# Ten added TensorE transposes of f32 words, two f16 numbers to a word, in the first stage of a matmul-logsumexp kernel

## The chip, the cores and the metric

The kernel runs on one core of one Trainium2 chip. The metric is device time in microseconds (us), as the median of several executions. One execution of each kernel is also taken by the hardware profiler; all numbers marked as read from the trace come from such a profile. The span in a profile (first to last instruction) is some 1.8 us shorter than the device time of the same execution.

## The reference

```python
m, k, n = 1024, 4096, 4096
a = np.random.randn(m, k).astype(np.float32)
b = np.random.randn(k, n).astype(np.float32)

def reference(a, b):
    x = np.matmul(a, b)
    return special.logsumexp(x, axis=-1).astype(np.float32)
```

## The kernel before

The kernel multiplies in f16 and works on blocks of 512 columns of b, most of them with a scheme of seven products in place of eight. Only the first stage matters here. In it, pieces of a (128 rows by 512 columns) and of b arrive by DMA, 64 arrivals in all, in groups of eight: a0, b, a1, b, a2, a3, a4, a5. Each piece of a is transposed on TensorE, four 128x128 transposes into one bank of PSUM (the memory that TensorE writes in this kernel, eight banks), and copied out to SBUF (the memory in which the operands lie), by VectorE and ScalarE in turn. There are two such banks, `tps[0]` and `tps[1]`, used in turn (`tps_99` and `tps_100` in the traces); the other six banks accumulate products.

```python
    tps = [
        psum_pool.tile([P, 2 * FD], f16, name=f"tps_{h}", tag="ps") for h in range(2)
    ]                                   # P = 128, FD = 512: each is one whole bank

    def transpose_group(k0, kn, m):     # kn = 4
        src = stg.pop((k0, m))
        n = count[0]                    # counts pieces of a only
        count[0] += 1
        pst = tps[n % 2]
        for j in range(kn):
            nc.tensor.matmul(pst[:, ts(j, P)], src[:, ts(j, P)], ident,
                             is_transpose=True, start=(j == 0), stop=(j == kn - 1))
        dst = aT[:, k0 // 2 : (k0 + kn) // 2, :, m // 2, m % 2, :]
        v = pst[:, 0 : kn * P].rearrange("p (i t c) -> p i t c", t=2, c=P)
        if n % 2 == 0:
            nc.vector.tensor_copy(out=dst, in_=v)     # L227
        else:
            nc.scalar.copy(out=dst, in_=v)            # L229

    # ... cut ...

    back = []
    for n, (k0, kn, what, x) in enumerate(arrivals):
        # ... issue of further loads, cut ...
        if what == "a":
            transpose_group(k0, kn, x)                # L216 in the profile
        if k0 < KN and x < 3:
            warm(1)                                   # matmuls of zeros, L295
        if len(back) == 1 + (n >= MT) + (n >= 4 * MT):
            behind(*back.pop(0))        # plain matmuls of an earlier arrival, L234,
        back.append((k0, kn, what, x))  # and sums of a on VectorE
        # ... cut ...

    # ... the other stages, cut ...
    nc.sync.dma_start(out=out.rearrange("(p mt) -> p mt", mt=MT), in_=lg)
```

The four transposes fill the lower half of a bank: 512 f16 of 1024. The upper half is free. In the traces of this kernel the matmuls, and the copies of each engine, run in the order in which the program names them.

Of the kernel before, what the change touches and what calls it, by code (L numbers as in the profile page):

```python
# [13 lines left out]
def kernel(  # L14
# [6 lines left out]
    nc = tc.nc  # L21
    P = 128
    FD = 512
    H = FD // 2
    f32 = mybir.dt.float32
    f16 = mybir.dt.float16
    AX = mybir.AxisListType
    ALU = mybir.AluOpType
# [6 lines left out]
    MP, KP = MT // 2, KT // 2  # L35
# [7 lines left out]
    cst_pool = ctx.enter_context(tc.tile_pool(name="cst", bufs=1))  # L43
# [14 lines left out]
            name=nc.get_next_instruction_name(),  # L58
# [7 lines left out]
    s1 = cst_pool.tile([P, KP, MP, P], f16, name="s1")  # L66
    s2 = cst_pool.tile([P, KP, MP, P], f16, name="s2")
# [15 lines left out]
    lg = cst_pool.tile([P, MT], f32, name="lg")  # L83
# [48 lines left out]
    class Block:  # L132
# [15 lines left out]
        def load(self, lo, hi):  # L148
            nc.gpsimd.dma_start(
                out=self.raw[lo // GI][:, lo % GI : lo % GI + hi - lo],  # L150
                in_=b_rows[:, lo:hi, :, ts(self.nb, FD)],
            )
# [36 lines left out]
    def acc_tiles(name):  # L189
# [6 lines left out]
    tps = [  # L196
        psum_pool.tile([P, 2 * FD], f16, name=f"tps_{h}", tag="ps") for h in range(2)
    ]
# [11 lines left out]
    def transpose_group(k0, kn, m):  # L210
        src = stg.pop((k0, m))
        n = count[0]
# [3 lines that stand above are left out]
            nc.tensor.matmul(  # L216
                pst[:, ts(j, P)],
                src[:, ts(j, P)],
                ident,
                is_transpose=True,  # L220
                start=(j == 0),
                stop=(j == kn - 1),
# [7 lines that stand above are left out]
# [40 lines left out]
    def behind(k0, kn, what, x):  # L270
        if what == "a":
            have_a.setdefault(k0, []).append(x)
            todo = [(k, x) for k in range(k0, k0 + kn) if k in have_b]
        else:
            have_b.update({k0: 1, k0 + 1: 1})
            todo = [(k, m) for k in (k0, k0 + 1) for m in have_a.get(x, [])]
        for k, m in todo:
            plain(acc[m // 2][m % 2], k // 2, k % 2, m)
        r = slice(k0 // 2, (k0 + kn) // 2)
        if what == "a":  # L280
            if x >= 3 and in_place:
                a_sums_late(*in_place.pop(0))
            if x % 2 == 1 and k0 + kn < KT:
                a_sums_early(r, x // 2)
            if x == 5:
                in_place.extend([(r, 0), (r, 1), (r, 2)])
            if k0 + kn == KT and x == 4:
                first_max(0)
                first_max(1)
                for what in ("t1", "t6"):  # L290
                    blk1.make(what, 0, 2)

    def warm(n):
        for _ in range(n):
            nc.tensor.matmul(acc[2][1], zeros[:, 0:P], zeros[:, 0:FD], start=True, stop=True)  # L295
# [21 lines left out]
    def load(k0, kn, what, x):  # L317
# [8 lines left out]
        if len(coming) == len(arrivals) - 3 * MT:  # L326
            nc.gpsimd.memset(negmax, 3.0e38)
            nc.gpsimd.memset(tsum, 0.0)

    back = []  # L330
    for n, (k0, kn, what, x) in enumerate(arrivals):
        while coming and (coming[0][2] == "b" or loads[0] < count[0] + NSLOT):
            load(*coming.pop(0))
            if not coming:
                for lo in range(0, KP, 2):
                    blk1.load(lo, lo + 2)
        if what == "a":
            transpose_group(k0, kn, x)
        if k0 < KN and x < 3:
            warm(1)  # L340
        if len(back) == 1 + (n >= MT) + (n >= 4 * MT):
            behind(*back.pop(0))
        back.append((k0, kn, what, x))
        while back and k0 < KN and what == "b":
            behind(*back.pop(0))
# [69 lines left out]
    def spread_turned():  # L415
        for g in range(4):
            for j in range(4):
                for eng, t, u in ((nc.gpsimd, tnm, negmax), (nc.gpsimd, tts, tsum)):
                    eng.tensor_copy(  # L419
                        out=u[ts(j, 32), :, WIDE[g]].rearrange("p (q r) -> p r q", r=2),  # L420
                        in_=t[ts(g, 32), 0].rearrange("p (r q j) -> p r q j", r=2, j=4)[
                            :, :, :, j
                        ],
                    )
# [86 lines left out]
    for step, (_, qs) in enumerate(plan):  # L511
# [4 lines left out]
        if more:  # L516
            if plan[step + 1][0] is again1:
                nxt = last
            else:
                nxt = plan[step + 1][0]()  # L520
                if step == 1:
# [3 lines left out]
                        out=ident[0:1, 0:2], in_=aT[0:1, 0, 0, MP - 1, :, 0]  # L525
# [23 lines left out]
        for q in qs:  # L549
# [108 lines left out]
            if final:  # L658
# [28 lines left out]
                    out=w, in_=w, func=AF.Exp, bias=n0, scale=-1.0, accum_out=l0  # L687
# [47 lines left out]
            if early and q == 1:  # L735
                last = again1().load_all()
                spread_turned()

    nc.sync.dma_start(out=out.rearrange("(p mt) -> p mt", mt=MT), in_=lg)


# [28 lines left out]
```

## Time and profile before

| | before |
|---|---|
| device time, median of the first 6 runs | 419.52 us (419.36 to 420.19) |
| span of the profile | 418.3 us |
| TensorE busy | 412.2 us |
| VectorE / ScalarE / GpSimd busy | 315.9 / 120.5 / 99.5 us |

The engines and their busy time, from the first part of the profile's page of the kernel before (PE is TensorE, PEld its weight loads, DVE VectorE, ACT ScalarE, POOL GpSimd), and the shares of the chain of work that ended last:

```profile
PE 412.2 (99%) x2747; PEld 261.4 (62%) x2747; DVE 315.9 (76%) x709; ACT 120.5 (29%) x447; POOL 99.5 (24%) x189
...
PE 97%; DMA 1%; DVE 0%; ACT 0%; issue 0%; SPq 0%; ACTq 0%
```

TensorE bounds the kernel. Its waits, longest first, in the kernel before (engine, what it was about to do, what it waited for; then us in total, times, longest):

```profile
PE acc_1_98 L295 <- DVE s_73 L298: 1.2, 1, 1.2
PE acc_0_93 L234 <- DVE aT L227: 0.6, 1, 0.6
```

Both are near the start. The stretch that the change touches comes next, as the timeline of the kernel before shows it (start, duration, engine, line, operation, output<-input, shapes, count; in brackets idle time before it and what ended it). A matmul's record ends later than the next one starts (the group of four at 27.15 has 0.39 us, and the next group starts 0.22 us after it); the text counts the distance of starts, the pitch.

```profile
27.15 0.39 PE L216 MATMUL tps_99<-ident,tb 128*128 128x128 f16 x4
...
27.37 1.03 PE L234 MATMUL acc_0_97<-b_1_86,aT 128*128 128x512 f16 x4
27.57 0.42 DVE L227 COPY aT<-tps_99 128x512 f16<-128x512 f16 x1 [0.74 <-PE tps_99 L216]
...
29.10 0.39 PE L216 MATMUL tps_100<-ident,tb 128*128 128x128 f16 x4
...
29.52 0.59 ACT L229 COPY aT<-tps_100 128x512 f16<-128x512 f16 x1 [2.45 <-PE tps_100 L216]
...
29.75 0.39 PE L216 MATMUL tps_99<-ident,tb 128*128 128x128 f16 x4
...
30.16 0.11 PEld L234 LDWEIGHTS <-aT 128*128 128x128 f16 x2 [0.19 <-ACT aT L229]
30.16 0.61 PE L234 MATMUL acc_1_94<-b_1_86,aT 128*128 128x512 f16 x2
```

Four f16 transposes take 0.22 us of pitch (27.15 to 27.37), 56 ns each. TensorE goes on at once with matmuls into other banks while VectorE copies the transposes out, until 27.99. The arrivals are 24 (27.15), 26 (29.10) and 28 (29.75); the two pieces of b between them have no transposes.

One more reading, on how the two halves of a bank are treated. First the kernel before near 116 us: c21 and c22 are the two halves of the bank `acc_1_1`. The record of the product into c21 ends at 116.04 (115.44 + 0.60); the copy L631 reads c21 alone and starts at 117.83.

```profile
115.44 0.60 PE L560 MATMUL acc_1_1_1348<-b_3_750,s_72 128*128 128x256 f16 x4
115.88 1.91 PE L560 MATMUL acc_1_1_1348<-tb,aT 128*128 128x256 f16 x16
...
117.83 0.37 ACT L631 COPY s_1_1349<-acc_1_1_1348 128x256 f32<-128x256 f32 x1 [2.86 <-PE acc_1_1_1348 L560]
```

Then the same in the last step, where c22 has a bank of its own:

```profile
405.41 1.91 PE L560 MATMUL acc_3_1_3992<-aT,s_72 128*128 128x256 f16 x16
...
407.16 1.91 PE L560 MATMUL c_3993<-tb,aT 128*128 128x256 f16 x16
407.40 0.37 ACT L631 COPY s_3_3994<-acc_3_1_3992 128x256 f32<-128x256 f32 x1 [1.20 <-PE acc_3_1_3992 L560]
```

In a shared bank the copy starts 1.79 us after the end of its own product, and 0.04 us after that of the product into the other half (115.88 + 1.91 = 117.79); with separate banks it starts 0.08 us after its own product (405.41 + 1.91 = 407.32). This program orders accesses by bank, not by address. The Trainium skill, "PSUM — Partial Sum Buffer", section "PSUM bank collisions raise a hardware error", says why a program is made so: two engines that touch one bank and the same 32 partitions at once raise an error, at different addresses too.

### The profile page before, as it was taken

Reading aid. Unit: us, or ns where it says so; the run is one execution under the profiler, and the core shown is the slowest. Engines: PE = TensorE matmul, PEld = TensorE weight load, DVE = VectorE, ACT = ScalarE, POOL = GpSimd, SP = SyncE. Lnnn points to the kernel's source line nnn. Section 1 sums busy time; section 2 is a strip of 40 time slices with the busy share of each in tenths; the row PEclk is TensorE's granted clock in tenths of the full one; section 3 lists DMA queues with packets and bytes.
Section 4 is the critical chain, followed back from the end, with each engine's and each line's share of the span. In section 5 each row is a group of like instructions: output and inputs, shape, how many; then the busy total and the mean of one; then the engine's idle time right before and its main releaser. Section 6 shows DMA issues by size and latency. Waiting matters only on the chain.

```text
span 418.3 us, 7100 instructions
## 1 busy us (share of the span) xinstructions
PE 412.2 (99%) x2747; PEld 261.4 (62%) x2747; DVE 315.9 (76%) x709; ACT 120.5 (29%) x447; POOL 99.5 (24%) x189
## 2 busy tenths in 40 slices
PE   8999999999999999999999999999999999999996
PEld 2555558888888844444444444444444468888885
DVE  2466688869646657978788896978789998299955
ACT  2222341132132210515215051512406052222124
POOL 7677753001010030013100031012200230294000
PEclk9999999999999999999999999999999999999999
DMA  9999999999999499103980089300990059699000
GB/s 183 203 202 204 203 205 207 207 207 215 190 191 179 68 163 207 33 2 48 208 148 0 2 135 207 60 1 8 201 195 2 0 86 207 112 192 207 6 2 0
DMA packets 57841, 53.28 MB, mean 127 GB/s; under 512 B 10192, under 2 KB 56912, under 8 KB 57808
## 3 DMA queue, kind: packets, MB, share of 16 engines
q0 software_dynamic: 48928, 49.95, 72.3%
q1 hardware_dynamic: 8880, 2.89, 4.2%
q8 instruction: 21, 0.34, 0.3%
q14 instruction: 12, 0.10, 0.1%
HBM read 100.66 MB, written 2.10 MB: 246 GB/s over the span
## 4 chain that ended last, share of the span: by engine, by line
PE 97%; DMA 1%; DVE 0%; ACT 0%; issue 0%; SPq 0%; ACTq 0%
PE acc_1_94 L234 2%; PE acc_0_93 L234 2%; PE acc_0_95 L234 2%; PE acc_1_0_1347 L560 2%; PE acc_1_0_767 L560 2%; PE acc_2_0_769 L560 2%; PE acc_0_0_765 L560 2%; PE acc_1_0_3395 L560 2%; PE acc_3_0_3851 L560 2%; PE acc_3_0_3715 L560 2%; PE acc_0_0_3263 L560 2%; PE acc_2_0_1482 L560 2%; PE acc_0_0_1215 L560 2%; PE acc_2_0_3579 L560 2%; PE acc_3_0_1615 L560 2%; PE wide_1_2_3078 L445 2%
## 5 line engine op out<-in xcount | busy, mean ns | idle before, releaser
L560 PEld LDWEIGHTS <-aT 128*128 128x128 f16 x832 | 81.4, 98 | 9.6
L445 PEld LDWEIGHTS <-tb 128*128 128x128 f16 x384 | 37.6, 98 | 45.1
L382 ACT ACTIVATE tb<-tb,ident 128x32 f32<-128x32 f32 x128 | 39.1, 306 | 6.4 <-DVE ident L379 6.4
L403 POOL TENSOR_TENSOR ident<-ident,tmin 128x96 f32<-128x96 f32 x8 | 3.1, 384 | 134.9 <-DVE tmin L405 134.9
L391 ACT ACTIVATE tb<-tb 128x512 f32<-128x512 f32 x8 | 5.0, 630 | 90.1 <-DVE tb L86 90.1
L205 POOL DMA_DIRECT2D tb<-in_a_dram x47 | 25.4, 544 | 7.1 <-issue 2.0
L234 PEld LDWEIGHTS <-aT 128*128 128x128 f16 x192 | 16.8, 99 | 15.2 <-DVE aT L227 1.8
L229 ACT COPY aT<-tps_100 128x512 f16<-128x512 f16 x24 | 14.1, 586 | 39.0 <-PE tps_100 L216 39.0
L227 DVE COPY aT<-tps_99 128x512 f16<-128x512 f16 x24 | 10.2, 425 | 19.7 <-PE tps_99 L216 19.7
L382 ACT ACTIVATION_READ_ACCUMULATOR tb<-tb,ident 128x1 f32 x128 | 23.9, 186 | 0.0
L216 PEld LDWEIGHTS <-tb 128*128 128x128 f16 x192 | 15.0, 100 | 12.5 <-DVE tb L309 1.0
L560 PEld LDWEIGHTS <-s_71 128*128 128x128 f16 x208 | 20.3, 98 | 2.8
L560 PEld LDWEIGHTS <-s_72 128*128 128x128 f16 x208 | 20.4, 98 | 2.4
L560 PEld LDWEIGHTS <-s_73 128*128 128x128 f16 x208 | 20.3, 98 | 2.4
L89 DVE TENSOR_TENSOR aT<-aT 128x256 f16<-128x256 f16 (+1 forms) x56 | 16.2, 343 | 0.0
L379 DVE TENSOR_REDUCE ident<-tb 128x16 f32<-128x512 f32 x16 | 11.0, 686 | 1.1
L86 DVE TENSOR_TENSOR s_71<-aT 128x256 f16<-128x256 f16 (+1 forms) x26 | 8.2, 316 | 2.5 <-ACT aT L229 2.2
L216 PE MATMUL tps_99<-ident,tb 128*128 128x128 f16 x96 | 9.5, 223 | 0.1
L216 PE MATMUL tps_100<-ident,tb 128*128 128x128 f16 x96 | 9.5, 223 | 0.0
L86 DVE TENSOR_TENSOR s_73<-aT 128x256 f16<-128x256 f16 (+1 forms) x26 | 8.3, 318 | 0.0
L86 DVE TENSOR_TENSOR s_72<-aT 128x256 f16<-128x256 f16 (+1 forms) x26 | 8.3, 317 | 0.0
L419 POOL COPY tsum<-tts 32x8 f32<-32x8 f32 x16 | 7.8, 486 | 0.0
(939 smaller groups left out, 966.7 us busy)
## 6 DMA issues: line engine op xcount, KB each, us to landing
tb<-in_a_dram POOLq DMA_DIRECT2D x47, 128.0 KB, 5.9
aT<-in_b_dram POOLq DMA_DIRECT2D x4, 1024.0 KB, 15.1
b_1_86<-in_b_dram POOLq DMA_DIRECT2D x4, 256.0 KB, 6.2
b_2_87<-in_b_dram POOLq DMA_DIRECT2D x4, 256.0 KB, 6.2
b_3_88<-in_b_dram POOLq DMA_DIRECT2D x4, 256.0 KB, 6.2
b_0_89<-in_b_dram POOLq DMA_DIRECT2D x2, 512.0 KB, 9.1
b_1_90<-in_b_dram POOLq DMA_DIRECT2D x2, 512.0 KB, 12.3
b_2_91<-in_b_dram POOLq DMA_DIRECT2D x2, 512.0 KB, 15.6
```

Source lines behind the costliest of these rows:

```text
L86: nc.vector.tensor_tensor(out=o, in0=x, in1=y, op=ALU.add)
L89: nc.vector.tensor_tensor(out=o, in0=x, in1=y, op=ALU.subtract)
L205: nc.gpsimd.dma_start(out=slot, in_=a_m[m, :, k0 * P : (k0 + kn) * P])
L216: nc.tensor.matmul(pst[:, ts(j, P)], src[:, ts(j, P)], ident, is_transpose=True, start=(j == 0), stop=(j == kn - 1),)
L227: nc.vector.tensor_copy(out=dst, in_=v)
L229: nc.scalar.copy(out=dst, in_=v)
L234: nc.tensor.matmul(pt, aT[:, i, kp, m // 2, m % 2, :], blk0.raw[i // GI][:, i % GI, kp, :], start=(done[m] == 0), stop=(done[m] == KT - 1),)
L379: nc.vector.tensor_reduce(out=nm, in_=v, axis=AX.X, op=ALU.max, negate=True)
L382: nc.scalar.activation(out=v[:, i], in_=v[:, i], func=AF.Exp, bias=nm[:, i : i + 1], accum_out=tts[:, 1 + h, r * WN // 2 + i : r * WN // 2 ...
L419: eng.tensor_copy(out=u[ts(j, 32), :, WIDE[g]].rearrange("p (q r) -> p r q", r=2), in_=t[ts(g, 32), 0].rearrange("p (r q j) -> p r q j", r ...
L445: nc.tensor.matmul(c.rearrange("p (q m) -> p q m", m=P), lhs(i), rhs(i), start=(start and i == 0), stop=(stop and i == KP - 1), skip_group ...
L560: nc.tensor.matmul(c, lhs(i), rhs(i), start=(start and i == 0), stop=(i == KP - 1), skip_group_check=True,)
```

## The change

The intent is to see what f32 transposes cost and whether they pass words unchanged. Each f32 word holds two f16 numbers, the lower 1.0 and the upper 0, so the word as an f32 is subnormal (all bits of its exponent are 0). At five arrivals two transposes of such words go into the upper half of a `tps` bank, and VectorE takes the minimum of the lower f16 numbers. At the end 1000 times that minimum less 1000 is added to the output: 0 if the words came through, far off if a lower number came out smaller. The check is narrower than the intent: each of the five reductions overwrites `seen`, so only the last, of arrival 28, reaches the output, and a minimum of the lower numbers shows neither one that came out larger nor a changed upper number.

```diff
+    word_id = s2[:, KP - 1].rearrange("p q c -> p (q c)").bitcast(f32)[:, 0:P]
+    words16 = s1[:, KP - 1].rearrange("p q c -> p (q c)")[:, 0 : 2 * P]
+    words = words16.bitcast(f32)
+    seen = cst_pool.tile([P, 1], f32, name="seen")
+
+    def words_through(n):
+        for j in range(2):
+            nc.tensor.matmul(
+                tps[n % 2].bitcast(f32)[:, 2 * P + j * P : 2 * P + (j + 1) * P],
+                words,
+                word_id,
+                is_transpose=True,
+                start=(j == 0),
+                stop=(j == 1),
+            )
+        v = tps[n % 2][:, 4 * P : 8 * P].rearrange("p (c t) -> p t c", t=2)
+        nc.vector.tensor_reduce(out=seen, in_=v[:, 0], axis=AX.X, op=ALU.min)
+
     back = []
     for n, (k0, kn, what, x) in enumerate(arrivals):
 ... cut ...
         if what == "a":
             transpose_group(k0, kn, x)
+        if n == 10:
+            make_identity(nc, word_id)
+            nc.vector.memset(words16, 0.0)
+            nc.vector.memset(words16[:, 0::2], 1.0)
+        if n in (24, 25, 26, 27, 28):
+            words_through(n)
 ... cut ...
+    nc.vector.tensor_scalar(
+        out=seen, in0=seen, scalar1=1000.0, scalar2=-1000.0, op0=ALU.mult, op1=ALU.add
+    )
+    nc.vector.tensor_scalar(
+        out=lg, in0=lg, scalar1=seen, scalar2=None, op0=ALU.add
+    )
     nc.sync.dma_start(out=out.rearrange("(p mt) -> p mt", mt=MT), in_=lg)
```

Note that `words_through` chooses its bank by the arrival's number, `transpose_group` by the count of pieces of a. So at arrivals 24 and 28 the words go into the bank that was just written and is about to be copied out; at 27 into the bank of arrival 26; at 25 and 26 into a bank that is free.

## The prediction

> **What bounds the kernel now.** TensorE. The chain of waits gives PE 97% of the span, the busy table 412.2 of 418.3 us. In the first stage (to about 62 us, 64 arrivals, a period of 6.72 us for eight) PE is solid: its waits are 1.2 and 0.6 us, both near the start. The added transposes fall in the fourth group of arrivals: by the order of matmuls in the timeline, between 27.15 and 30.6 us. Nothing later has slack, so what PE loses there moves the end one for one.
>
> **What is added, in order of size.**
>
> 1. Waits on PE. The added transposes write the upper half of a bank whose lower half is being copied out. The trace shows that the halves of a bank are ordered against each other in this program: the ScalarE copy of c21 (L631) could start when its own product ends (115.9 us), yet starts at 117.83, after the product into the other half of the bank; in the last step, where that product has its own bank, the copy starts at once (407.40 after 407.32). So I expect:
>    - arrival 24: after its four transposes the words wait for VectorE's copy of the same bank. PE would go on at 27.37; the copy ends at 27.99: about 0.67 us.
>    - arrival 28: the same, 0.67 us.
>    - arrival 27: waits for ScalarE's copy of arrival 26 (29.52 + 0.59 us): 0.84 us less the words of arrival 26. It swallows the wait of 0.19 us that is now at 30.16.
>    - arrivals 25 and 26: their banks should be free.
>    Sum: 0.67 + 0.67 + 0.84 - 0.19 = 2.0 us, less one pair of words.
> 2. The transposes. An f16 transpose has 56 ns of pitch here (four in 0.22 us). The Trainium skill, "TensorE: Matmul & The Clock Gate", Terms, says that trn2's transpose mode made FP32 four times faster, so I take one pass; its section on weight-path modes says that fast weight load is not for FP32, so the weight load (98 ns busy for f16 here) may set the pitch. Estimate: 0.12 us each, a pair w = 0.25 us. Five pairs less the one hidden: 4w = 1.0 us. No f32 matmul is in this trace. Four passes would make it 2 us or more.
> 3. Changes between f32 and f16 weights: 0.2 us, a guess.
> 4. The tail: two small VectorE instructions, the second dependent on the first, before the store. Such ones step by 0.19 us there (412.51 to 412.70). Together 0.3 us, on the chain.
>
> Off the chain: five reductions of 256 f16 from PSUM (about 0.4 us each, as the 128x256 one at 413.43), where VectorE has 4.3 us busy of 6.8; two memsets; the identity on GpSimd, 0.5 to 0.9 us, in gaps of its load issue. Nothing is removed.
>
> **Prediction.** 419.5 + 2.0 + 1.0 + 0.2 + 0.3 = 423.0 us, range 421.3 to 425.3. Faster by over 2%: 0.01; within 2%: 0.95; slower by over 2%: 0.04.
>
> The words are subnormal as f32. I expect them through unchanged (3 in 4); otherwise the output is off by 1000, at the same time.
>
> **Right if** the waits of PE show two of about 0.65 us for VectorE's L227 copies and one of about 0.6 us for ScalarE's L229 copy; the ten matmuls pitch at 60 to 130 ns; the tail is 0.3 us longer; all between keeps its length.
>
> **Wrong if** the halves of a bank are not ordered (421.3 us or less), f32 transposes take several passes or stall the weight load (over 425), or the reductions delay VectorE's copies so that later transposes wait.

## More of the kernel before

The end of the kernel before:

```profile
415.81 0.16 DVE L89 TENSOR_TENSOR lg<-lg,nmmin 128x2 f32<-128x2 f32 x1 [0.65 <-ACT lg L689]
416.00 0.35 SPq L739 DMA_DIRECT2D out_dram<-lg  x1
```

## The result, and the profile after

The changed kernel is correct. Its median is 422.66 us (422.35 to 423.93, 10 runs) against 419.62 us (418.95 to 421.06, 20 runs) of the kernel before: 3.04 us more. The ratio is 1.0074, with a 95% interval of 1.0063 to 1.0085, so 2.6 to 3.6 us.

The stretches of the two kernels, from the windows view. The first window runs from the start of the transposes of arrival 24 to the first matmul after the first stage; the second from there to the end of TensorE's work. Columns: start and end, length, then busy us (and instructions) of each engine, granted clock, DMA share, GB/s. Before:

```profile
27.15:61.67 34.52, 34.50 (x249) 19.22 (x248) 23.79 (x94) 10.44 (x20) 23.52 (x39) 1.00 1.24 204
61.67:414.35 352.68, 352.64 (x2353) 230.01 (x2351) 279.76 (x568) 101.72 (x412) 55.91 (x110) 1.00 0.70 116
```

After:

```profile
26.05:63.68 37.63, 36.05 (x259) 20.39 (x258) 25.81 (x99) 10.42 (x20) 25.10 (x41) 1.00 1.24 204
63.68:416.36 352.68, 352.64 (x2353) 230.00 (x2351) 279.45 (x568) 101.71 (x412) 55.56 (x110) 1.00 0.69 115
```

The first window is 3.11 us longer (37.63 - 34.52). All that follows up to the tail has the same length to 10 ns. TensorE has 1.58 us of idle time in the first window where it had 0.02.

The same stretch of the timeline, now of the changed kernel:

```profile
26.47 0.42 DVE L227 COPY aT<-tps_99 128x512 f16<-128x512 f16 x1 [0.74 <-PE tps_99 L216]
...
27.05 0.41 PE L337 MATMUL tps_99<-s_72,s_71 128*128 128x128 f32 x2 [0.61 <-DVE aT L227]
...
27.29 1.03 PE L234 MATMUL acc_0_97<-b_1_86,aT 128*128 128x512 f16 x4
...
28.16 0.38 PE L337 MATMUL tps_100<-s_72,s_71 128*128 128x128 f32 x2
...
29.24 0.39 PE L216 MATMUL tps_100<-ident,tb 128*128 128x128 f16 x4
...
29.46 0.39 PE L337 MATMUL tps_99<-s_72,s_71 128*128 128x128 f32 x2
...
29.66 0.58 ACT L229 COPY aT<-tps_100 128x512 f16<-128x512 f16 x1 [3.69 <-PE tps_100 L216]
...
30.30 0.44 PE L337 MATMUL tps_100<-s_72,s_71 128*128 128x128 f32 x2 [0.45 <-ACT aT L229]
...
30.57 0.59 PE L234 MATMUL acc_0_93<-b_1_86,aT 128*128 128x512 f16 x2
...
31.00 0.39 PE L216 MATMUL tps_99<-ident,tb 128*128 128x128 f16 x4
31.43 0.42 DVE L227 COPY aT<-tps_99 128x512 f16<-128x512 f16 x1 [0.17 <-PE tps_99 L216]
...
31.91 0.44 PE L337 MATMUL tps_99<-s_72,s_71 128*128 128x128 f32 x2 [0.52 <-DVE aT L227]
...
32.19 0.59 PE L234 MATMUL acc_1_94<-b_1_86,aT 128*128 128x512 f16 x2
```

The added transposes are L337. At arrival 24 (transposes from 26.05, four of them, so TensorE could go on at 26.27) the words start at 27.05, after VectorE's copy ended at 26.89: 0.78 us lost. At arrival 27 the words could start at 29.46 + 0.22 = 29.68, and start at 30.30, after ScalarE's copy: 0.62 us. At arrival 28 they could start at 31.22 and start at 31.91: 0.69 us. The old wait of 0.19 us before L234 is gone, because ScalarE's copy was waited for already. The sum is 0.78 + 0.62 + 0.69 - 0.19 = 1.90 us. The five pairs themselves take 0.24, 0.21, 0.22, 0.27 and 0.28 us from their start to the next matmul, 1.22 us (the third, behind which TensorE waits, is put at 0.22 us like the pairs in the flow). 1.90 + 1.22 = 3.12 us, which accounts for the 3.11.

The same trace holds the counterpart. The pair of arrival 26 (29.46) also comes directly behind four transposes whose copy is still to come, but goes into the other bank, which nobody reads then: it starts 0.22 us after them, without a wait. The pair of arrival 25 (28.16), whose bank is free too, does not wait either. Only the pairs whose own bank was still to be copied out waited.

The bracket of a wait is shorter (0.61, 0.45, 0.52) than the time lost, because the modelled end of the matmul before it counts as busy. The waits view of the changed kernel has the same numbers:

```profile
PE tps_99 L337 <- DVE aT L227: 1.1, 2, 0.6
PE tps_99 L216 <- DMA tb<-in_a_dram: 1.0, 2, 0.7
...
PE tps_100 L337 <- ACT aT L229: 0.5, 1, 0.5
```

Its second line is one that the profile of before did not have: transposes that waited for loads of a (`tb` holds the staged pieces). It is taken up below.

The tail of the changed kernel:

```profile
417.81 0.16 DVE L89 TENSOR_TENSOR lg<-lg,nmmin 128x2 f32<-128x2 f32 x1 [0.65 <-ACT lg L713]
417.89 0.15 DVE L763 TENSOR_SCALAR seen<-seen 128x1 f32<-128x1 f32 x1
418.07 0.23 DVE L766 TENSOR_SCALAR lg<-lg,seen 128x8 f32<-128x8 f32 x1
418.40 0.35 SPq L769 DMA_DIRECT2D out_dram<-lg  x1
```

The store follows the last subtraction by 0.59 us in place of 0.19: 0.40 us more.

So the traces say 3.11 + 0.40 = 3.51 us, and the times say 3.04 us with an interval that reaches to 3.6. The spans of the two profiles differ by only 2.4 us (420.7 - 418.3), because the changed kernel came to arrival 24 earlier by 1.10 us (26.05 against 27.15). This is not the change's doing: in the second profile of the kernel before (the last experiment) arrival 24 starts at 26.14 us, and against its span of 417.3 us the changed kernel has 3.4 us more.

### The profile page after: what moved, and what is told of

Read it like the earlier page. It is cut to its first block, busy times and chain, and to the rows that moved or that the text cites. A ratio compares the mean times of both kernels' runs of the same rounds, so it can differ in the third digit from the quotient of the medians. Undisturbed runs are those within 1.5% of the kernel's fastest.

```text
span 420.7 us, 7137 instructions
## 1 busy us (share of the span) xinstructions
PE 411.6 (98%) x2757; PEld 261.7 (62%) x2757; DVE 318.4 (76%) x718; ACT 120.5 (29%) x447; POOL 100.4 (24%) x191
## 4 chain that ended last, share of the span: by engine, by line
PE 93%; DMA 4%; DVE 0%; POOL 0%; issue 0%; ACT 0%; POOLq 0%; ACTq 0%
DMA tb<-in_a_dram 3%; PE acc_1_0_1369 L584 2%; PE acc_1_0_789 L584 2%; PE acc_0_0_787 L584 2%; PE acc_2_0_791 L584 2%; PE acc_3_0_3873 L584 2%; PE acc_2_0_3601 L584 2%; PE acc_1_0_3417 L584 2%; PE acc_0_0_3285 L584 2%; PE acc_3_0_3737 L584 2%; PE acc_3_0_1637 L584 2%; PE acc_2_0_1504 L584 2%; PE acc_0_0_1237 L584 2%; PE wide_1_1_1971 L469 2%; PE wide_1_2_3100 L469 2%; PE wide_1_0_2722 L469 2%
## 5 line engine op out<-in xcount | busy, mean ns | idle before, releaser
L234 PEld LDWEIGHTS <-aT 128*128 128x128 f16 x192 | 16.8, 98 | 13.4 <-DVE aT L227 1.3
```

What stands on the lines that cost most here:

```text
L234: nc.tensor.matmul(pt, aT[:, i, kp, m // 2, m % 2, :], blk0.raw[i // GI][:, i % GI, kp, :], start=(done[m] == 0), stop=(done[m] == KT - 1),)
```

## The experiments

Theory A, mine: the larger part of the loss is TensorE waiting for copies out of a bank that it is to write again, the smaller part the transposes themselves at one pass (one streaming of their 128 columns) each. Rivals: B, the f32 transposes themselves are the cost (several passes); C, the set-up delays the loads; D, the reductions hold up VectorE's copies. Later L: the first stage is paced by loads here and there, and a loss of TensorE is partly handed back there; R denies it.

The table gives the length of the first window (from the start of arrival 24's transposes, or of the words where they come ahead of them, to the first matmul after the first stage), read from each trace, and beside it the median time less that of the kernel before of the same rounds.

| kernel | first window, us | over before, us | ratio, 95% interval |
|---|---|---|---|
| before (two profiles) | 34.52, 34.53 | 0 | |
| change | 37.63 | 3.04 | 1.0063 to 1.0085 |
| tail only | 35.26 | 0.52 | 1.0005 to 1.0032 |
| no tail | 37.64 | 2.57 | 1.0054 to 1.0080 |
| words ahead of the transposes | 35.47 | 0.90 | 1.0014 to 1.0040 |
| eight at each arrival | 40.26 | 5.70 | 1.0126 to 1.0154 |
| before, TensorE made late | 34.53 | 1.56 | 1.0032 to 1.0073 |
| change, TensorE made late | 37.64 | 5.41 | 1.0113 to 1.0152 |
| f16 in place of f32 | 36.95 | 2.88 | 1.0055 to 1.0079 |
| one reduction | 37.63 | 3.44 | 1.0072 to 1.0098 |

### Tail only

```diff
-        if n in (24, 25, 26, 27, 28):
-            words_through(n)
+            nc.vector.memset(seen, 1.0)        # under n == 10
```

> No added transposes and no reductions; identity, memsets and the two last VectorE instructions stay. Theory A (waits for the copies of the shared bank are the largest part): 0.3 to 0.4 us over the kernel before, all of it in the tail. Theory B (the f32 transposes themselves are the cost): the same 0.3 to 0.4. Theory C (the set-up on GpSimd and VectorE delays the loads): over 0.8 us.

Measured: 420.19 us (419.73 to 420.84) against 419.67 us, 0.52 us over; the trace has the tail 0.39 us longer than before, as in the change. Theory C is not supported: by the medians the set-up costs what is left, 0.1 us, which is within the noise. The interval (0.2 to 1.3 us) does not exclude C's 0.8 us by itself; the traces say more. In the changed kernel the identity (GpSimd, 19.93 to 20.64 us) puts one issue of a load of a at 20.71 us, where both profiles of the kernel before have it at 20.14; by the semaphore updates in the traces that load lands at 26.23 us, against 26.07 and 26.37, and the last load of a at 56.00 us, against 55.82 and 56.13. So the set-up does not delay the loads there. The time missed the stated 0.3 to 0.4 us by 0.1. This trace has a longer first window, 35.26 us, for want of loads (its last load of a lands at 56.31 us): TensorE comes to arrival 24 at 25.63 us, earlier than in any other run. Waits for loads are also found in the kernel before (see the last experiment), though there before arrival 24 only.

### The change without its tail

The two last VectorE instructions are taken out.

> The change without its two last VectorE instructions. If the parts simply add: 2.6 to 2.8 us over the kernel before. If the local loss that the trace of the change shows (3.1 us between arrivals 24 and 29) is not recovered at all: 3.1 us.

Measured: 422.24 us (421.83 to 422.90), 2.57 us over. The first window is 37.64 us, the whole loss of 3.11 us. Together with the tail alone, 2.57 + 0.52 = 3.09 us: the parts add up to the 3.04 us of the change. The interval (2.3 to 3.4 us) contains both of the expected numbers, so this run does not decide whether the whole local loss shows.

### The words ahead of the ordinary transposes

```diff
+        added = n in (24, 26, 28, 29, 30)      # pieces of a only
+        bank = count[0]                        # the bank that the transposes take next
+        if added:
+            words_through(bank)                # the two matmuls alone
         if what == "a":
             transpose_group(k0, kn, x)
+        if added:
+            look(bank)                         # the reduction, after the copy
```

> Ten f32 transposes and five reductions as in the change, but each pair just ahead of the four ordinary transposes into the same bank, and its reduction after the copy, so that no pair waits for a copy of its own bank. Theory A: the waits go, five pairs of 0.25 us and the tail stay, 1.5 to 1.8 us over the kernel before, and the waits of PE list no wait of the added transposes over 0.2 us. Theory B: still about 3.0 us over. Theory D (the reductions hold up the copies on VectorE): still 2.5 us or more, with waits of later matmuls for VectorE's copies.

Measured: 420.57 us (420.39 to 421.02), 0.90 us over. The pairs go with pieces of a alone, so three of the five arrivals are others than in the change. The same ten transposes and five reductions cost 2.1 us less. The waits of TensorE's matmuls name no L337 at all (one of its weight loads waited 0.3 us for a reduction, under a matmul that was still running). The timeline of this run shows how the pair now goes through (tile numbers are left out in this trace):

```profile
26.06 0.38 PE L337 MATMUL tps<-s,s 128*128 128x128 f32 x2
26.28 0.39 PE L216 MATMUL tps<-ident,tb 128*128 128x128 f16 x4
26.50 1.89 PE L234 MATMUL acc<-b,aT 128*128 128x512 f16 x8
26.70 0.42 DVE L227 COPY aT<-tps 128x512 f16<-128x512 f16 x1 [0.96 <-PE tps L216]
```

The pair takes 0.22 us and nothing waits. Theories B and D are refuted. The stated 1.5 to 1.8 us was too high: I had put 0.25 us on each pair, which contains the restart after a wait, and had forgotten that the old wait of 0.19 us is filled here too. By the trace, 0.95 us in the first window and 0.40 in the tail make 1.35; the time is lower still, by 0.45 us, and the interval (0.6 to 1.7 us) contains both.

### Eight transposes at each arrival

`for j in range(2)` becomes `for r in range(8)` with `j = r % 2`: the same two places are written four times.

> Eight f32 transposes in place of two at each of the five arrivals, 30 more. Theory A: one pass and a pitch of 0.11 to 0.13 us, so 3.3 to 3.9 us above the change, less up to 0.7 us that the longer work at arrival 26 takes out of the wait at arrival 27: 6.0 to 6.9 us over the kernel before. Theory B (several passes, 0.25 us or more each): 7.5 us above the change or more.

Measured: 425.37 us (425.35 to 425.59), 5.70 us over, so 2.7 us above the change for 30 more transposes. The lower end was missed by 0.3 us. The pitch can be read without any wait:

```profile
29.03 1.04 PE L338 MATMUL tps<-s,s 128*128 128x128 f32 x8
29.91 1.03 PE L234 MATMUL acc<-b,aT 128*128 128x512 f16 x4
```

Eight take 0.88 us, 0.11 us each, twice the f16 pitch of 56 ns, and the trace has one instruction for each transpose. In the first window the 30 cost 40.26 - 37.63 = 2.63 us; 30 x 0.11 = 3.3 us, less the 0.62 us that TensorE no longer waits at arrival 27, because the longer work of arrival 26 covers ScalarE's copy. So theory B's several passes of 0.25 us or more for each transpose are refuted, and the waits are there beside the transposes. Whether the 0.11 us are one pass at half the pace or two at that of f16, no run shows.

### f16 transposes in the same places

```diff
-                tps[n % 2].bitcast(f32)[:, 2 * P + j * P : 2 * P + (j + 1) * P],
-                words,
-                word_id,
+                tps[n % 2][:, 4 * P + j * P : 4 * P + (j + 1) * P],
+                words16[:, 0:P],
+                ident,
 ... the reduction and a memset, adapted to f16, cut ...
```

> f16 transposes in place of the f32 ones, in the same places and the same bank, with the same waits. Theory A: three waits of the added transposes as in the change (about 0.5 us each), and four exposed pairs at 0.11 in place of 0.25 us: 2.4 to 2.7 us over the kernel before. Theory B (f32 is the cost): 1 us or less.

Measured: 422.21 us (421.91 to 422.57), 2.88 us over, a little above what was stated. The trace agrees with theory A: read as above, the waits cost 0.68 + 0.72 + 0.69 - 0.19 = 1.90 us, as in the change, and the five pairs 0.11 us each, 0.55 us; the first window is 2.42 us longer than before. The waits of TensorE in this run, of the added transposes:

```profile
PE tps L337 <- DVE aT L227: 1.0, 2, 0.5
PE tps L337 <- ACT aT L229: 0.6, 1, 0.6
```

One thing differs: at arrival 24 the f32 words start 0.15 us after the end of the copy, in all eight runs with f32 words behind the transposes of that arrival. At arrivals 27 and 28, where they wait, they start 0.05 us after it, as the f16 ones do at all three. Why the first f32 pair takes 0.1 us more there stays open. f32 accounts for 37.63 - 36.95 = 0.68 us of the 3.11. The rest comes with any transposes in these places.

### One reduction in place of five

The reduction is left out at arrivals 24 to 27.

> The change with only the last of its five reductions. Theory A: the reductions are off the chain, so the same as the change within 0.2 us: 2.8 to 3.2 us over the kernel before. Theory D (they hold up VectorE's copies): 0.5 us or more below the change.

Measured: 422.77 us (422.63 to 423.86), 3.44 us over; first window 37.63 us, the same as the change to 10 ns. The reductions are off the chain. The time is above the stated 2.8 to 3.2 us; it is also above the change's, with less work. Equal traces and times that differ by 0.4 us show how well such differences can be read between two rounds.

### TensorE made late, without and with the change

```diff
         if k0 < KN and x < 3:
             warm(1)
+        if n == 6:
+            warm(12)                           # twelve matmuls of zeros
```

> The kernel before with twelve more matmuls of zeros after the sixth arrival (2.6 us of TensorE at full clock), so that TensorE is behind the loads for the rest of the first stage. Theory L (in most executions TensorE waits for loads of a here and there in the first stage, and a loss there shortens later waits of that kind): no waits for loads in the trace after the added matmuls, and 0.9 to 1.6 us over the kernel before, less than the 2.6 us added. Rival R (nothing in the stage is paced by loads): 2.6 us over.

> The change with the same twelve matmuls. What counts is the distance to the run just before. Theory L: the whole local loss and the tail show, 3.1 + 0.4 = 3.5 us. Rival R (the loss is handed back somewhere else): 3.0 us as between the change and the kernel before.

Measured: 420.89 us (420.45 to 423.25) for the kernel before with this, 1.56 us over, by the ratio 2.2 us (two of its six runs are near 423); 424.74 us (424.12 to 426.77) for the change with this. In the first trace the twelve matmuls add 2.59 us (from 10.14 to 13.82 us between two groups of transposes, where other runs have 1.09), and no wait for a load is left. By the medians only 1.56 us of them show: this supports theory L's half that the start of the first stage is in part paced by loads. It does not show it, since the ratio's interval (1.3 to 3.1 us) also contains the full 2.6.

The other half stays open. The distance of the two is 3.85 us by the medians and 3.3 us by the ratios (0.79% of 420 us), around the 3.5 us of theory L, and not clear of the 3.0 us of R. Both first windows are what they were, 34.53 and 37.64 us.

### One word of zero

`nc.vector.memset(words16[32:33, 10:11], 0.0)` follows the other memsets.

> Wrong on purpose: one word of the 16384 (row 32, column 5) is zero. If the output shows any change in the words, as is meant, the eight outputs of partition 5 are 1000 too low and all others right. If the check is blind, the result is right. Same time as the change.

Measured: wrong, relative error 0.38008 (one execution, 423.54 us). Eight outputs off by 1000 give sqrt(8) x 1000 / 7441.7 = 0.38008, where 7441.7 is the norm of the reference's output, worked out with numpy from the fixed draw of the inputs. So one zero word of 16384 moves eight outputs; the check that the change makes of its own words is not blind to a lower number that comes out smaller. (The number does not say which eight.)

### Random pairs through two transposes

```diff
+        pair = src[:, 0 : 2 * P]               # staged a: two random f16 in each word
+        transpose(out32[:, 2 * P : 3 * P], pair.bitcast(f32), word_id)
+        nc.vector.tensor_copy(out=words16, in_=tps[n % 2][:, 4 * P : 6 * P])
+        transpose(out32[:, 3 * P : 4 * P], words, word_id)
+        nc.vector.tensor_tensor(out=words16, in0=tps[n % 2][:, 6 * P : 8 * P],
+                                in1=pair, op=ALU.not_equal)
+        nc.vector.tensor_reduce(out=seen, in_=words16, axis=AX.X, op=ALU.max)
```

(`transpose` stands for the matmul call with `is_transpose`; at arrival 24 only, and the tail adds 1000 times `seen`.)

> In place of the words: 256 columns of staged a data (two random f16 numbers in each f32 word) go through one f32 transpose, are copied out, go through a second one and are compared with the source; any f16 that differs moves the output by 1000. If transposes pass every bit of a word: a right result. If the f32 path rounds a word's low bits: wrong by 1000 in all or nearly all outputs.

Measured: correct. 32768 random f16 numbers, in pairs in ordinary f32 words, came back equal after two f32 transposes. No run shows that this comparison would fire, only that the same tail does.

### Half the streamed columns

Eight at each arrival, with `words[0 : P // 2]` and a 64x64 identity.

> Forty f32 transposes as in the run with eight per arrival, but of 64 rows with a 64x64 identity, so that 64 and not 128 columns stream; the weight load keeps its 128 columns. If the weight load sets the pitch of 0.11 us, it stays 0.11; if the streaming does, it falls to 0.055 to 0.06.

Measured: the wait-free eight went from 28.50 to 29.15 us in the trace, 0.08 us each, between the two expectations. The number of rows was halved as well as that of streamed columns, so this run does not tell what sets the pitch. It is inconclusive.

### The kernel before once more

> The kernel before once more, for a second profile. Theory L: unless the clock of TensorE rises as late as in the first profile (matmuls of zeros and plain ones 0.43 us apart until 10.4 us), the stage to 62 us shows waits of the transposes for loads, 0.5 to 1.7 us in all. Rival R: no such waits.

Measured: 419.12 us, span 417.3 us. Its waits have this line:

```profile
PE tps L216 <- DMA tb<-in_a_dram: 0.8, 2, 0.4
```

The kernel before does wait for loads, as theory L stated. Its first profile had been one with a slow start. There, plain matmuls of 512 columns are 0.43 us apart until 10.4 us:

```profile
9.10 0.63 PE L234 MATMUL acc_0_93<-b_0_85,aT 128*128 128x512 f16 x1
9.53 0.63 PE L234 MATMUL acc_1_94<-b_0_85,aT 128*128 128x512 f16 x1
```

In the second one four of them from 8.05 us take until 8.91 us, 0.215 us each:

```profile
8.05 1.02 PE L234 MATMUL acc<-b,aT 128*128 128x512 f16 x4 [0.19 <-DMA b<-in_b_dram]
8.91 0.39 PE L216 MATMUL tps<-ident,tb 128*128 128x128 f16 x4
```

The Trainium skill, "TensorE: Matmul & The Clock Gate", Part 1, gives 426.7 ns for such a matmul at half clock and 215.7 ns at full clock, and says that the moment of the rise differs from run to run; the two traces agree with both. In each trace the record of the granted clock begins with the rise to full clock, at 10.43 us in the first profile and at 3.96 in the second. In the three traces where it comes at 7.2 us or later, no transposes wait for loads (one of these three is the change with TensorE made late); of the eleven where it comes by 6.7 us, ten have such waits, and the eleventh is the kernel before with TensorE made late. So in these traces TensorE with a late rise is behind the loads, and with an early one it runs into them. In this second profile both waits of the transposes end before arrival 24 (at 15.16 and 22.22 us), and the first window has its 34.53 us. In the profile of the tail alone there are two such waits after arrival 24 too, at 41.37 and 56.12 us: 0.4 us by the waits view, 0.7 us by the length of the first window.

## Why the prediction was right

It said 423.0 us, and 422.66 us was measured. The terms of its sum, against the traces:

| term | predicted, us | in the traces, us |
|---|---|---|
| waits for copies of the same bank, less the old wait | 2.0 less one pair = 1.75 | 0.78 + 0.62 + 0.69 - 0.19 = 1.90 |
| the five pairs | 5 x 0.25 = 1.25 | 1.22 |
| changes between f32 and f16 | 0.2 | none of its own (0.1 at arrival 24, counted in the waits, may be one) |
| tail | 0.3 | 0.40 |
| sum | 3.5 | 3.5 |

That the two sums agree so closely is luck: the guess of 0.2 us fell away, and the waits and the tail were 0.15 and 0.10 us longer than stated. The terms themselves held.

- That the halves of a bank are ordered was read from the trace of before, from one copy that started 1.79 us after the record of its product ended. The three waits came where it put them, and the run without them (words ahead of the transposes) lost 2.1 us of the 3.0.
- The wait at arrival 24 was 0.11 us longer than stated, the others within 0.03 us of it. The restart after a wait costs 0.02 to 0.06 us more than a pair of 0.22 us in the flow; in the flow it is 0.11 us a transpose.
- One pass for an f32 transpose rested on the Trainium skill, "TensorE: Matmul & The Clock Gate", Terms. The trace agrees with the time worked out from it: one matmul instruction of 0.11 us pitch for each, where 0.12 us was stated. Against f16 it is twice the time, so the number of passes is not shown, and no run has an f32 matmul that is not a transpose, so the factor of four is not shown either.
- "All between keeps its length" holds to 10 ns (352.68 us in both).
- The words came through unchanged as far as the check looks: no lower number of the last pair came out smaller. The random pairs were compared in full.
- One statement was wrong: that in the first stage "PE is solid" and that nothing there has slack. That was true of the one profile at hand, whose clock rose late. Most of the other traces have waits of 0.3 to 1.9 us for loads of a in that stage, the second one of the kernel before 0.8 us. It is a possible reason why the time grew by 3.04 and not by 3.5 us, but it is not shown: the intervals of the runs contain both numbers, and the pair of runs made for it did not part them.

## What to carry to other kernels

In this program an instruction that writes the free half of a bank waits for whoever reads the other half: before putting work into spare PSUM space, look at what the last instruction on that bank is, and place the work ahead of the write that will be read, not after it; here this turned 3.0 us into 0.9. Whether work meets such a wait depends on the bank and not on its place alone: arrival 26's pair, behind transposes into the other bank, did not wait. An f32 transpose passed two f16 numbers in each word intact in all that was compared here, but takes twice as long as an f16 one (0.11 us against 56 ns), so packing pairs saves instructions and not TensorE time. Take a second profile before calling a stage free of waits: two profiles of the same kernel, with early and late rise of TensorE's clock, came to arrival 24 at 26.14 and 27.15 us, one with waits for loads and one without.

## What the Trainium skill lacked or had wrong

- "TensorE: Matmul & The Clock Gate", Terms, says only that transpose mode made FP32 four times faster. The runs show the pitch: 0.11 us for a 128x128 f32 transpose in a stream, 56 ns for an f16 one, with weight loads of 140 and 98 ns.
- The same page, Part 4, gives about 390 ns for a 128x128 bf16 transpose in isolation and about 275 ns in one kernel. In this one an f16 transpose has 219 ns in the record and a pitch of 56 ns.
- No page speaks of subnormal words or pairs of f16 in an f32 transpose. Two come near it: "PSUM — Partial Sum Buffer", Specifications, says that transposes write the input's type uncast, and "Perfetto Trace Analysis", Transposes, that they skip arithmetic. Here 16384 random pairs came back equal after two transposes; of the 16384 words with the pattern of 1.0 below 0, no lower half came out smaller.
- "PSUM — Partial Sum Buffer", section "PSUM bank collisions raise a hardware error", says that accesses of different engines to one bank and the same 32 partitions are to be ordered; it has no figure for what that costs. Here a transpose behind a copy of its bank waits 0.62 to 0.78 us for a copy of 0.42 (VectorE) or 0.58 us (ScalarE).
